# A decoder layer in fp32 on one core: casts begun one unit ahead, some low parts made by accumulating transfers, and eleven activations per feed-forward turned by transposing transfers

## The chip, the core and the metric

The kernel runs on one core of one Trainium2 chip. A core has five engines with their own instruction queues that meet through semaphores: TensorE (PE: matrix products; its weight loads are shown apart as PEld), VectorE (DVE), ScalarE (ACT), GpSimd (POOL) and SyncE (SP, which here only issues transfers). Sixteen DMA engines move data between device memory and on-chip memory, and between places in on-chip memory. The metric is device time of one execution in microseconds. All times are in us unless marked ns.

## The reference

One layer for 256 tokens of 2048 features, in float32:

```python
h = layer_norm(alpha * x + 0.5 * swiglu(x, w_ffn1_gu, w_ffn1_down))         # ffn 1, 2048 -> 2 x 5632 -> 2048
rq, rk, rv, rg, aq, ak, av, gate_r, gate_a = split(h @ w_in)
ret = (silu(rg) * group_norm(retention(rotary(rq), rotary(rk), rv))) @ w_ret_out
att = sliding_window_attention_with_sinks(rotary(aq), rotary(ak), av) @ w_att_out
h = layer_norm(alpha * h + (sigmoid(gate_r) * ret + sigmoid(gate_a) * att) @ w_mix_out)
h = layer_norm(alpha * h + 0.5 * swiglu(h, w_ffn2_gu, w_ffn2_down))         # ffn 2
h = layer_norm(alpha * h + sigmoid(h @ w_ple_gate) * (p @ w_ple_proj))
# swiglu(x, w_gu, w_down): g, u = split(x @ w_gu); return (silu(g) * u) @ w_down
```

Nearly all the work is products of 256 tokens with large weight matrices that are read once.

## The kernel before

**Three products for one.** Each fp32 operand is split into a high part (a cast to the type fp32r, `act.copy`, on ScalarE) and a low part (operand less high part, `dve.tensor_tensor`, on VectorE). `Sum.add` (L370 to L379) then issues three matmuls: low × high (L377), high × high (L378), high × low (L379).

**Units.** Weights come in chunks of 128 × 1024 floats (512 KB) by transfers from SP (L112). A plain unit (`Single`, "P", two per pair of chunks) is one chunk: load, cast (L98), subtraction (L99), then 12 matmuls of 512 columns. An S unit (`Seven`) takes a pair of chunks through Strassen's scheme: seven products for eight, 21 matmuls, for which VectorE forms four sums and more low parts (L174 to L185). A D unit (`Prepared`) has those sums written to device memory earlier, by VectorE in quieter stages (`sums_ahead`), and loads them.

**The planner.** `plan` lists the units in order. `fill` (L263) loads the next one while there is room in a budget of slots (`room["slots"]`, 24 in the feed-forwards' first products) and less than 90 matmuls are queued, and makes the next loaded one (cast and low parts) while less than 45 matmuls are ready. `take` hands a unit to TensorE, `done` gives its slots back and calls `fill`. Engines execute in the order in which the code is traced; a transfer also waits until the slot it writes has been released. All slots come from one pool of 46 of 4 KB per partition.

**Side jobs.** `later(n, job)` puts a job n places down a list; `run_side`, called after each chunk or S unit, runs the first entry. So `later(3, job)` runs behind the fourth next chunk.

**A feed-forward** (`ffn`, L898). The first product is done in 11 blocks of 512 columns (256 gate, 256 up). Block 0 has 16 plain chunks; the others follow an order of eight pairs, `PPSSPSSP` for ffn 1 (L860), with D units in blocks 1, 2, 3, 4, 5 and 7 of ffn 2 (L859). Four PSUM banks (`g`, `u`) collect the direct products and four more (`s0` to `s3`) Strassen's sums. Behind the last S unit `seven_common` (L479) folds the latter on VectorE (L483 to L486), a last plain pair follows, then VectorE adds the direct sums (L972), ScalarE applies Silu (L973) and VectorE multiplies (L974, by `later(1)`) into a tile `evw` of [128 tokens, 2, 512]. The down projection needs it transposed: `turned` (L908, by `later(2)`) transposes eight 128 × 128 squares on TensorE (L916) into two PSUM banks and copies them out by ScalarE (L918). `convert` (L922) splits the result, `seven_forms` makes sums of it; both are used from block 10 on.

**Between the feed-forwards** lies the mixer. Its value product uses the order `PSPSPSPS` (L1084); behind it the q and k projections of retention (`rqk`, L1178 to L1181) begin, whose matmuls stand at L328 (high) and L336 (low).

Of the kernel before, what the change touches and what calls it, by code (L numbers as in the profile page):

```python
# [10 lines left out]
I32 = mybir.dt.int32  # L11
AF = mybir.ActivationFunctionType
# [3 lines left out]
P = 128  # L16
S = 256
# [38 lines left out]
def layer(ctx: ExitStack, tc: tile.TileContext, io):  # L56
# [44 lines left out]
    class Chunk:  # L101
# [18 lines left out]
        def make(self):  # L120
            self.make_hi()
            split(self.hi, self.lo, self.raw)
# [6 lines left out]

        def columns(self, kk):  # L130
            return self.of(self.hi, kk), self.of(self.lo, kk)

    class Single:
# [9 lines left out]

        def make(self):
            self.chunk.make()

    class Seven:
# [4 lines left out]
        loads, makes, keeps, time = 2, 6, 7, 21  # L152
# [6 lines left out]

        def make(self):  # L160
# [4 lines left out]

            def shaped(x):
                return x.rearrange("p (g n) -> p g n", g=2) if a.paired else x

            t1, t3, t2, t4 = (shaped(x) for x in (u[:, 0], u[:, 1], v[:, 0], v[:, 1]))
            a.make_hi()  # L170
            both = slot([P, 2, 512], F32R, "b" + nm)
            h22, l22 = shaped(both[:, 0]), shaped(both[:, 1])
            uh, ul, vh, vl = (slot([P, 2, 512], F32R, w + nm) for w in ("hu", "lu", "hv", "lv"))
            act.copy(a.hi, a.raw)  # L174
            act.copy(h22, b22)
# [4 lines left out]
            dve.tensor_tensor(a.lo, a.raw, a.hi, ALU.subtract)  # L180
            dve.tensor_tensor(t4, t2, b21, ALU.add)  # L181
            act.copy(vh, v)  # L182
            dve.tensor_tensor(l22, b22, h22, ALU.subtract)
            dve.tensor_tensor(ul, u, uh, ALU.subtract)  # L184
            dve.tensor_tensor(vl, v, vh, ALU.subtract)  # L185
            self.b11, self.b21 = a.columns(0), a.columns(1)
            self.b22 = both[:, 0], both[:, 1]
# [5 lines left out]
    class Prepared:  # L193
# [3 lines left out]

        def __init__(self, key, other):
            self.key, self.other = key, other
# [10 lines left out]

        def make(self):
            a = self.a
            a.make()
            self.b11, self.b21 = a.columns(0), a.columns(1)
            both = slot([P, 2, 512], F32R, "b" + a.name)
            self.b22 = both[:, 0], both[:, 1]
            split(*(both[:, e].rearrange("p (g n) -> p g n", g=2) for e in range(2)), self.b)
            uh, ul, vh, vl = self.sums
            self.t1, self.t3 = ((uh[:, e], ul[:, e]) for e in range(2))
            self.t2, self.t4 = ((vh[:, e], vl[:, e]) for e in range(2))  # L220
# [42 lines left out]
    def fill(must=False):  # L263

        while True:
            queued = sum(u.time for u in ready)
            left = room["slots"] - room["used"]
            wanted = must and not ready or not room["quiet"] and queued < room["ahead"]
            if loaded and wanted and loaded[0].makes <= left:
                u = loaded.pop(0)  # L270
                u.make()
                room["used"] += u.keeps - u.loads
                ready.append(u)
                continue
            first = loaded[0] if loaded else plan[0] if plan else None
            queued += sum(u.time for u in loaded)
            if plan and queued < room["far"] and plan[0].loads + first.makes <= left:
                u = plan.pop(0)
                u.load()
                room["used"] += u.loads  # L280
                loaded.append(u)
                continue
            return

    def make_next():
        u = loaded.pop(0)
        assert u.makes <= room["slots"] - room["used"]
        u.make()
        room["used"] += u.keeps - u.loads
# [109 lines left out]
    def block_units(units, keys):  # L399

        for kind, p in units:
            if kind == "P":
                plan.extend(Single(keys(n, p)) for n in range(2))
# [3 lines left out]
    def block(name, units, keys, lhs, forms, sums, fold, before=None):  # L407


        sevens = [p for kind, p in units if kind != "P"]  # L410
        if sevens:
            p1, p6, p7, q5 = (Sum(bank(f"{name}s{j}"), len(sevens)) for j in range(4))
        for j, (kind, p) in enumerate(units):
            if before is not None:
                before(j)
            if kind == "P":
# [21 lines left out]
            if p == sevens[-1]:  # L438
                fold(p1.ap, p6.ap, p7.ap, q5.ap)

# [26 lines left out]
    def units_of(order, sevens, ahead=()):  # L467
# [3 lines left out]
        of = {"S": sevens, "D": ahead, "P": plain}  # L471
# [383 lines left out]
    def gu_units(name, j):  # L855
# [4 lines left out]
        return units_of("PPSSPSSP", SEVEN)  # L860
# [37 lines left out]
    def ffn(name, i, ht, norm, keep, residual, keepers, away):  # L898
# [9 lines left out]
        def turned(j, v):  # L908

            raw = slot([P, 4, S], F32, f"{name}a{j}")  # L910
            raws.append(raw)
            ps = banks(f"{name}t{j}")
            for k in range(4):
                for t in range(2):
                    at = slice(k % 2 * S + t * P, k % 2 * S + t * P + P)
                    pe.transpose(ps[k // 2][:, at], v[:, t, k * P : (k + 1) * P], ident)  # L916
            for h in range(2):
                act.copy(raw[:, 2 * h : 2 * h + 2], ps[h].rearrange("p (b n) -> p b n", b=2))  # L918
# [8 lines left out]
        for j in range(KF // 4):  # L927
            pg, pu = banks(f"{name}g{j}"), banks(f"{name}u{j}")
            units = gu_units(name, j)
            n_of = {(0, 0): KD, (0, 1): KD, (1, 0): KD, (1, 1): KD}  # L930
            for kind, p in units:
                if kind != "P":
# [34 lines left out]
            block(f"{name}{j}", units, gu_keys(name, j), rhs, forms, sums, lambda *a: got.extend(seven_common(*a)), before)  # L967
# [13 lines left out]
            later(2, lambda j=j, v=v: turned(j, v))  # L981
# [102 lines left out]
    VALUE_UNITS = units_of("PSPSPSPS", (0, 1, 2, 3))  # L1084
# [32 lines left out]
    def mixers(ht, norm, residual, keepers, away):  # L1117
# [57 lines left out]
        slots_for_weights(14)  # L1175
        rq[:] = [slot([P, 4, S], F32, f"rq{j}") for j in range(2)]
# [630 lines left out]
```

## Time and profile before

| | |
|---|---|
| three runs | 2278.32 median, 2276.88 to 2278.9 |
| the profiled execution | 2278.22, span of its instructions 2276.4 |
| granted TensorE clock, mean | 0.998 |
| PE / DVE / ACT / POOL busy | 2260.9 / 2031.3 / 1241.1 / 2.3 |
| matmuls | 10467 |
| moved by DMA | 515.72 MB, nearly all on SP's queue |

The profile is of one execution. A matmul's duration in it (0.39 us for 512 columns) overlaps with the next one's; the distance between starts says what one costs. "idle before" and "<-" name the time that an engine stood before an instruction and what ended it. Tile names are cut of their numbers: `f1g` are the gate sums of ffn 1, `f1t` the banks of a turn, `hf_gu` and `lf_gu` the high and low part of a chunk, `rf_gu` the chunk as loaded, `huf_gu`, `hvf_gu` and `luf_gu`, `lvf_gu` the parts of an S unit's sums. A row of stretches gives, between two times, busy time and instructions of each engine, the granted clock, the DMA engines' busy share and GB/s.

### The profile page before, as it was taken

To read this page: it belongs to the slowest core of one execution; us is meant where nothing else is said; L and a number is where in the kernel's file an instruction comes from. 1 tells how busy PE (TensorE), PEld (TensorE's weight loads), DVE (VectorE), ACT (ScalarE), POOL (GpSimd) and SP (SyncE) were. 2 spreads that over 40 slices of the span, in tenths; PEclk is the share of its full clock that TensorE was granted. 3 is DMA by queue.
4 is the path that set the end of the run, shared out by engine and by line. 5 is a ranking of instruction groups with operands and counts; after the bars stand their busy time and mean duration, and the time that the engine had idled before them with its cause. 6 is when DMAs were issued, how large, how long until landed. Compare 5 with 4: busy or idle time off the path is not lost.

```text
span 2276.4 us, 29157 instructions
## 1 busy us (share of the span) xinstructions
PE 2260.9 (99%) x10467; PEld 1873.9 (82%) x10467; DVE 2031.3 (89%) x2664; ACT 1241.1 (55%) x1514; POOL 2.3 (0%) x9
## 2 busy tenths in 40 slices
PE   9999999999999999999999999999999999999998
PEld 8888888888888888888778888888888888888887
DVE  7999999999989999888789788689898899889887
ACT  5655655656554644445666544455555556555543
POOL 0000000000000000000000000000000000000000
PEclk9999999999999999999999999999999999999999
DMA  8666665665677778866446568787877766556772
GB/s 309 207 197 196 196 213 176 198 209 190 212 286 263 258 243 309 269 225 217 147 148 223 193 208 293 271 286 253 287 260 226 254 206 205 194 188 215 290 270 74
DMA packets 211129, 515.72 MB, mean 227 GB/s; under 512 B 16412, under 2 KB 20892, under 8 KB 210984
## 3 DMA queue, kind: packets, MB, share of 16 engines
q1 hardware_dynamic: 209000, 511.28, 66.4%
q10 hardware_dynamic: 1984, 2.58, 0.4%
q8 instruction: 82, 1.34, 0.2%
q14 instruction: 63, 0.52, 0.1%
HBM read 484.43 MB, written 29.36 MB: 226 GB/s over the span
## 4 chain that ended last, share of the span: by engine, by line
PE 91%; DVE 8%; issue 1%; ACT 0%; ACTq 0%; POOL 0%; DVEq 0%; POOLq 0%
PE rqk L328 3%; PE f1g L379 2%; PE f1g L377 2%; PE f1g L378 2%; PE f2g L379 2%; PE f2g L378 2%; PE f1u L379 2%; PE f2g L377 2%; PE f1u L377 2%; PE f1u L378 2%; PE f2u L379 2%; PE f2u L377 2%; PE f2u L378 2%; PE aqk L328 2%; PE f2d L379 2%; PE f1d L378 2%
## 5 line engine op out<-in xcount | busy, mean ns | idle before, releaser
L99 DVE TENSOR_TENSOR lf_gu<-rf_gu,hf_gu 128x1024 fp32r<-128x1024 f32 (+1 forms) x192 | 223.7, 1210 | 15.2 <-ACT hf_gu L98 14.6
L98 ACT CAST hf_gu<-rf_gu 128x1024 fp32r<-128x1024 f32 (+1 forms) x192 | 190.3, 1041 | 20.7 <-DMA rf_gu<-in_f_gu 19.0
L99 DVE TENSOR_TENSOR lw_in_f<-rw_in_f,hw_in_f 128x1024 fp32r<-128x1024 f32 x132 | 158.0, 1219 | 25.1 <-ACT hw_in_f L98 24.9
L99 DVE TENSOR_TENSOR lf_down<-rf_down,hf_down 128x1024 fp32r<-128x1024 f32 x124 | 147.3, 1221 | 25.4 <-ACT hf_down L98 24.9
L98 ACT CAST hf_down<-rf_down 128x1024 fp32r<-128x1024 f32 x124 | 125.2, 1049 | 34.9 <-DMA rf_down<-in_f_down 15.4
L179 ACT CAST huf_gu<-uf_gu 128x1024 fp32r<-128x1024 f32 x76 | 80.1, 1054 | 109.5 <-DVE uf_gu L177 79.4
L98 ACT CAST hw_in_f<-rw_in_f 128x1024 fp32r<-128x1024 f32 x132 | 132.8, 1051 | 9.8 <-DMA rw_in_f<-in_w_in_f 3.1
L182 ACT CAST hvf_gu<-vf_gu 128x1024 fp32r<-128x1024 f32 x76 | 80.1, 1054 | 96.9 <-DVE vf_gu L181 93.0
L184 DVE TENSOR_TENSOR luf_gu<-uf_gu,huf_gu 128x1024 fp32r<-128x1024 f32 x76 | 92.7, 1220 | 0.0
L185 DVE TENSOR_TENSOR lvf_gu<-vf_gu,hvf_gu 128x1024 fp32r<-128x1024 f32 x76 | 92.7, 1220 | 0.0
L180 DVE TENSOR_TENSOR lf_gu<-rf_gu,hf_gu 128x1024 fp32r<-128x1024 f32 x76 | 92.7, 1220 | 0.0
L377 PE MATMUL f1g<-hf_gu,xt 128*128 128x512 f32 x232 | 90.4, 390 | 0.0
L379 PE MATMUL f1g<-lf_gu,xt 128*128 128x512 f32 x232 | 90.4, 389 | 0.0
L378 PE MATMUL f1g<-hf_gu,xt 128*128 128x512 f32 x232 | 90.3, 389 | 0.0
L973 ACT ACTIVATE eve<-eve 128x1024 f32<-128x1024 f32 x20 | 21.2, 1061 | 114.9 <-DVE eve L972 114.9
L377 PE MATMUL f2g<-hf_gu,ht 128*128 128x512 f32 x214 | 83.5, 390 | 0.0
L379 PE MATMUL f2g<-lf_gu,ht 128*128 128x512 f32 x214 | 83.3, 389 | 0.0
L378 PE MATMUL f2g<-hf_gu,ht 128*128 128x512 f32 x214 | 83.3, 389 | 0.0
L174 ACT CAST hf_gu<-rf_gu 128x1024 fp32r<-128x1024 f32 x76 | 79.6, 1047 | 4.0 <-DMA rf_gu<-in_f_gu 4.0
L377 PE MATMUL f1u<-hf_gu,xt 128*128 128x512 f32 x192 | 75.6, 394 | 0.0
L379 PE MATMUL f1u<-lf_gu,xt 128*128 128x512 f32 x192 | 74.8, 390 | 0.0
L378 PE MATMUL f1u<-hf_gu,xt 128*128 128x512 f32 x192 | 74.8, 389 | 0.0
(1572 smaller groups left out, 6865.7 us busy)
## 6 DMA issues: line engine op xcount, KB each, us to landing
rf_gu<-in_f_gu SPq DMA_DIRECT2D x360, 512.0 KB
rf_down<-in_f_down SPq DMA_DIRECT2D x176, 512.0 KB
rw_in_f<-in_w_in_f SPq DMA_DIRECT2D x148, 512.0 KB
rw_rv<-in_w_rv SPq DMA_DIRECT2D x32, 512.0 KB
rw_ret<-in_w_ret SPq DMA_DIRECT2D x32, 512.0 KB
rw_mix<-in_w_mix SPq DMA_DIRECT2D x32, 512.0 KB
rw_pg<-in_w_pg SPq DMA_DIRECT2D x32, 512.0 KB
rw_att<-in_w_att SPq DMA_DIRECT2D x16, 512.0 KB
```

What stands on the lines that cost most here:

```text
L98: act.copy(dst_hi, src)
L99: (lo_engine or dve).tensor_tensor(dst_lo, src, dst_hi, ALU.subtract)
L174: act.copy(a.hi, a.raw)
L179: act.copy(uh, u)
L180: dve.tensor_tensor(a.lo, a.raw, a.hi, ALU.subtract)
L182: act.copy(vh, v)
L184: dve.tensor_tensor(ul, u, uh, ALU.subtract)
L185: dve.tensor_tensor(vl, v, vh, ALU.subtract)
L328: pe.matmul(ps[f], hi[:, kk, f * P : (f + 1) * P], rhs(k), start=k == 0, stop=k == n_k - 1,)
L377: pe.matmul(o, al, bh, start=first, stop=False)
L378: pe.matmul(o, ah, bh, start=False, stop=False)
L379: pe.matmul(o, ah, bl, start=False, stop=self.left == 0)
```

## The change

1. **Casts one unit ahead.** A unit gets a step `begin` ahead of `make`: the casts of the chunks as loaded. `make_next` begins the unit at hand if that has not been done, then the next one (a T unit already when it is third in line) if there are slots, and then makes its low parts.
2. **T units.** In the orders without D units, `PPSSPSSP` becomes `PTSSPSST`. The second chunk of a T pair is `Transferred`: ScalarE writes the negated high part into the low part's slot, and a transfer from GpSimd's queue adds the chunk to it in place, which leaves the low part; the cast to the high part comes in `make`.
3. **Turns.** `turned` now copies the tile's 16-bit halves apart on ScalarE (`later(3)`); `turn`, three steps on, issues one transposing transfer of 128 × 2048 two-byte elements from SP; `join`, four steps on, copies the halves together on ScalarE. No transposes on TensorE and no PSUM banks.
4. **Banks and the value block.** For even blocks from 2 the four banks of Strassen's sums are asked for ahead of `g` and `u`. The value product's order becomes `PSPSSPSP`, and four banks named `pass` are asked for, and not used, behind it.

```diff
     class Chunk:
-        def make(self):
-            self.make_hi()
-            split(self.hi, self.lo, self.raw)
+        def begin(self):
+            self.hi = slot(list(self.raw.shape), F32R, "h" + self.name)
+            act.copy(self.hi, self.raw)
+        def end(self):
+            self.lo = slot(list(self.raw.shape), F32R, "l" + self.name)
+            dve.tensor_tensor(self.lo, self.raw, self.hi, ALU.subtract)
+        def transfer(self):
+            self.lo = slot(list(self.raw.shape), F32R, "l" + self.name)
+            act.mul(self.lo, self.raw, -1.0)
+            pool.dma_start(self.lo, self.raw.bitcast(F32R), accum_op=ALU.add)
...
+    class Unit:
+        begun, begins, lead = False, 1, 1
...
+    class Transferred(Single):
+        lead = 3
+        def begin(self):
+            self.chunk.transfer()
+        def make(self):
+            self.chunk.begin()
...
     class Seven(Unit):
+        def begin(self):
+            a, b = self.a, self.b
+            a.begin()
+            self.both = slot([P, 2, 512], F32R, "b" + a.name)
+            self.h22, self.l22 = (a.shaped(self.both[:, e]) for e in range(2))
+            act.copy(self.h22, b.of(b.raw, 1))
...
+    def begin(u):
+        u.begun = True
+        u.begin()
+        u.loads, u.makes = u.loads + u.begins, u.makes - u.begins
+        room["used"] += u.begins
+
     def make_next():
         u = loaded.pop(0)
         assert u.makes <= room["slots"] - room["used"]
+        if not u.begun:
+            begin(u)
+        room["used"] += u.keeps - u.loads
+        for j, v in enumerate(loaded[:3]):
+            if not v.begun and j < v.lead and v.begins + (loaded[0].makes if j else 0) <= room["slots"] - room["used"]:
+                begin(v)
         u.make()
-        room["used"] += u.keeps - u.loads
         ready.append(u)
...
-        return units_of("PPSSPSSP", SEVEN)
+        return units_of("PTSSPSST", SEVEN)
...
         def turned(j, v):
+            parts = slot([P, 2, 2, 512], U16, f"{name}w{j}")
+            words = v.bitcast(U16).rearrange("p t (n w) -> p w t n", w=2)
+            for w in range(2):
+                act.copy(parts[:, w], words[:, w])
+            later(3, lambda: turn(j, parts))
+
+        def turn(j, parts):
+            turns = slot([P, 16, P], U16, f"{name}t{j}")
+            sync.dma_start_transpose(turns, parts.rearrange("p w t n -> p (w t n)"))
+            later(4, lambda: join(j, turns))
+
+        def join(j, turns):
             raw = slot([P, 4, S], F32, f"{name}a{j}")
             raws.append(raw)
-            ps = banks(f"{name}t{j}")
-            for k in range(4):
-                for t in range(2):
-                    at = slice(k % 2 * S + t * P, k % 2 * S + t * P + P)
-                    pe.transpose(ps[k // 2][:, at], v[:, t, k * P : (k + 1) * P], ident)
-            for h in range(2):
-                act.copy(raw[:, 2 * h : 2 * h + 2], ps[h].rearrange("p (b n) -> p b n", b=2))
+            words = raw.bitcast(U16).rearrange("p k (t n w) -> p w k t n", t=2, w=2)
+            turns = turns.rearrange("p (w t k) n -> p w k t n", w=2, t=2)
+            for w in range(2):
+                act.copy(words[:, w], turns[:, w])
...
+            extra = seven_banks(f"{name}{j}") if j and j % 2 == 0 else None
             pg, pu = banks(f"{name}g{j}"), banks(f"{name}u{j}")
...
-            later(2, lambda j=j, v=v: turned(j, v))
+            later(3, lambda j=j, v=v: turned(j, v))
...
-    VALUE_UNITS = units_of("PSPSPSPS", (0, 1, 2, 3))
+    VALUE_UNITS = units_of("PSPSSPSP", (0, 1, 2, 3))
...
         slots_for_weights(14)
+        for j in range(4):
+            bank(f"pass{j}")
```

More of the change, by code (lines that the diff above doesn't have):

```diff
@@ L11 @@
 I32 = mybir.dt.int32
+U16 = mybir.dt.uint16
 AF = mybir.ActivationFunctionType
@@ L965, in before @@
                     convert(u // 2 - 2)
[L967 removed]
+            block(f"{name}{j}", units, gu_keys(name, j), rhs, forms, sums, lambda *a: got.extend(seven_common(*a)), before, extra)
             if got:
```

76 lines of the change are left out of this document (36 added, 40 removed).

## The prediction

> **What bounds the kernel now.** I read the page first, then who made TensorE wait, then the instructions around one turn in order of time, then the stretches of the first feed-forward.
>
> ```profile
> span 2276.4 us, 29157 instructions
> ...
> PE 2260.9 (99%) x10467; PEld 1873.9 (82%) x10467; DVE 2031.3 (89%) x2664; ACT 1241.1 (55%) x1514; POOL 2.3 (0%) x9
> ...
> q1 hardware_dynamic: 209000, 511.28, 66.4%
> ...
> PE 91%; DVE 8%; issue 1%; ACT 0%; ACTq 0%; POOL 0%; DVEq 0%; POOLq 0%
> ```
>
> TensorE is busy for all but 15.5 us of the span and is 91% of the chain that ended last. A gain must therefore come from fewer or shorter TensorE instructions, and every other engine only has to keep up. The list of TensorE's waits is short:
>
> ```profile
> PE rqk L328 <- DVE evw L483: 2.8, 1, 2.8
> PE f2t L916 <- DVE evw L974: 2.4, 9, 0.3
> PE f1t L916 <- DVE evw L974: 2.4, 9, 0.3
> ```
>
> Two of the three rows are the transposes of `turned` (L916), which the change takes off TensorE; the third is the start of the q and k projections behind the value block, whose order it alters. In order of time, a turn in a later block of the first feed-forward (start, duration):
>
> ```profile
> 182.11 0.39 PE L379 MATMUL f1g<-lf_gu,xt 128*128 128x512 f32 x1
> ...
> 183.47 0.39 PE L379 MATMUL f1g<-lf_gu,xt 128*128 128x512 f32 x1
> 184.13 1.07 PE L916 MATMUL f1t<-ident,evw 128*128 128x128 f32 x8 [0.27 <-DVE evw L974]
> 184.95 0.48 PE L377 MATMUL f1u<-hf_gu,xt 128*128 128x512 f32 x1
> 185.27 0.39 PE L378 MATMUL f1u<-hf_gu,xt 128*128 128x512 f32 x1
> ```
>
> and one without the wait, for block 0:
>
> ```profile
> 57.43 0.39 PE L379 MATMUL f1g<-lf_gu,xt 128*128 128x512 f32 x1
> 57.66 1.03 PE L916 MATMUL f1t<-ident,f1v 128*128 128x128 f32 x8
> 58.45 0.47 PE L377 MATMUL f1u<-hf_gu,xt 128*128 128x512 f32 x1
> 58.77 0.39 PE L378 MATMUL f1u<-hf_gu,xt 128*128 128x512 f32 x1
> ```
>
> Durations overlap, so cost is read from starts. Six matmuls take 183.47 − 182.11 = 1.36, or 0.2267 us each. Around the first turn, L379 to L378 takes 185.27 − 183.47 = 1.80 us where two intervals would take 0.45: the turn costs **1.35 us**. Without the wait it is 58.77 − 57.43 − 0.45 = **0.89 us**.
>
> What must keep up, by stretches (length; then busy us of PE, PEld, DVE, ACT, POOL; granted clock; DMA share; GB/s):
>
> ```profile
> 139.60:181.80 42.20, 41.93 (x190) 34.59 (x189) 41.16 (x50) 24.54 (x29) 0.00 (x0) 1.00 0.62 188
> 181.80:223.90 42.10, 41.83 (x190) 34.47 (x189) 41.05 (x50) 24.38 (x29) 0.00 (x0) 1.00 0.61 188
> ...
> 1573.00:1614.00 41.00, 40.74 (x184) 33.59 (x183) 40.09 (x50) 23.52 (x28) 0.00 (x0) 1.00 0.82 291
> 1614.00:1656.00 42.00, 41.73 (x189) 34.38 (x189) 36.69 (x44) 22.99 (x28) 0.00 (x0) 1.00 0.73 248
> ```
>
> The first two are one block of ffn 1 each: VectorE works 41.1 of 42.2 us. It runs only a little ahead of TensorE. The last low part of a block's fourth S unit is made, and used, here:
>
> ```profile
> 204.60 1.22 DVE L185 TENSOR_TENSOR lvf_gu<-vf_gu,hvf_gu 128x1024 fp32r<-128x1024 f32 x1
> ```
>
> ```profile
> 209.32 0.39 PE L379 MATMUL f14s<-lvf_gu,f1fh 128*128 128x512 f32 x1
> ```
>
> It ends at 205.82, 3.5 us before its use: that is the smallest lead in a block.
>
> **The change part by part.**
>
> *Turns.* There are 22 (11 blocks in each ffn). 18 run behind `evw` (two rows of 9 waits), 4 without a wait (blocks 0 and 10 of each ffn, counted at block 0's price). TensorE loses 18 × 1.35 + 4 × 0.89 = 24.3 + 3.6 = **27.9 us** of work. Nothing on the chain takes its place if the new route is in time, since the results are first read in the last block (`convert`) and in the down projection.
>
> The new route costs ScalarE four copies of 1024 two-byte elements in place of two of 512 floats, and SP one transposing transfer:
>
> ```profile
> L98 ACT CAST hf_gu<-rf_gu 128x1024 fp32r<-128x1024 f32 x64 | 63.2, 1051 | 0.0
> L182 ACT CAST hvf_gu<-vf_gu 128x1024 fp32r<-128x1024 f32 x32 | 33.8, 1055 | 41.1 <-DVE vf_gu L181 41.1
> L179 ACT CAST huf_gu<-uf_gu 128x1024 fp32r<-128x1024 f32 x32 | 33.7, 1054 | 50.3 <-DVE uf_gu L177 33.9 <-PE f1t L916 16.4
> ...
> L918 ACT COPY f1a<-f1t 128x512 f32<-128x512 f32 x16 | 8.5, 584 | 0.0
> L973 ACT ACTIVATE eve<-eve 128x1024 f32<-128x1024 f32 x8 | 8.5, 1061 | 45.8 <-DVE eve L972 45.8
> ```
>
> (ScalarE in eight blocks: count, busy, mean ns, idle before, by whom.) No row has a two-byte copy; 584 ns (half the elements) and 1051 ns (as many) bound it, and I take 1.05. Each block then has 4.2 − 1.2 = +3.0 us of ScalarE. The split waits for `evw` on ScalarE; behind it stand only casts of later units, and the wait that L179 had for the transposes (16.4 us) goes.
>
> The transposing transfer moves 512 KB. Queue 1 carries 511.28 MB in 66.4% of 16 engines over 2276.4 us, which is 24,184 engine-us, 47.3 per MB: 512 KB alone on 16 engines is 24.8 / 16 = 1.55 us. That is the low end. For the high end let it be cut into 2048 pieces that each cost a mean packet of that queue, 24,184 / 209,000 = 0.116 us: 2048 × 0.116 / 16 = 14.8 us, and 39 us if it only gets the 0.38 of the engines that a block leaves idle. I take 4 us, nearer the low end because the bytes are the same. Its cover is the way from `turn` (behind the eighth chunk step) to `join` (the thirteenth): S, S, T, T, P are 21 + 21 + 12 + 12 + 12 = 78 matmuls, 17.7 us. SP's loads queue behind it while it waits for the split, but the split is traced 66 matmuls (15 us) earlier, so I charge nothing; unmet, each load behind it comes late by the remaining wait.
>
> [...]
>
> *Transferred chunks.* T units stand in ten blocks of ffn 1 and four of ffn 2 (blocks 6, 8, 9, 10): 28 chunks. Each takes one subtraction of 1024 columns off VectorE:
>
> ```profile
> L99 DVE TENSOR_TENSOR lf_gu<-rf_gu,hf_gu 128x1024 fp32r<-128x1024 f32 x8 | 9.3, 1220 | 0.2 <-ACT hf_gu L98 0.2
> ```
>
> 9.3 / 8 = 1.16 us, so 2.3 us a block: VectorE goes to 38.8 against a TensorE block of 42.2 − 1.35 = 40.8. ScalarE gains two scalings of 1.05 us (with the copies: 24.5 + 3.0 + 2.1 = 29.6 of 40.8), POOL two issues on an empty queue. The six ahead-blocks of ffn 2 have no T; there VectorE needs (40.09 + 36.69) / 2 = 38.4 per pair member against about 41.5 − 1.35 = 40.1, so it keeps up as well.
>
> The accumulating transfer reads source and destination and writes: one to three passes of 512 KB, 1.55 to 4.65 us alone, 12.2 us if it gets only the idle 0.38. I take 6. Followed through `take`, `fill` and `make_next` with 24 slots, a block's two T chunks are begun 60 and 66 matmuls before their first matmul; less the scaling that is 12.5 and 13.9 us, **13.2 on average**. Even the high end fits, barely. Cost: nothing; uncovered, L379 waits.
>
> *Casts one unit ahead.* VectorE's waits for its casts vanish, but TensorE's waits list shows none that they caused: nothing. The casts ask for their load 12 or 21 matmuls (2.7 or 4.8 us) earlier; the L98 row above has 0.0 idle, so the loads have been early enough by some margin that no row states. From nothing to ScalarE standing 2 us a block, inside its idle time; priced in the second rival.
>
> *Value block and banks.* The fold gets a plain pair behind it. Before:
>
> ```profile
> 796.08 3.49 DVE L99 TENSOR_TENSOR lw_in_f<-rw_in_f,hw_in_f 128x1024 fp32r<-128x1024 f32 x3
> ...
> 800.22 2.79 PE L328 MATMUL rqk<-ht,hw_in_f 128*128 128x512 f32 x7 [2.76 <-DVE evw L483]
> ```
>
> ```profile
> 760.00:815.00 55.00, 51.46 (x235) 42.27 (x234) 54.59 (x69) 31.64 (x37) 0.00 (x0) 0.97 0.82 283
> ...
> 801.00:804.30 3.30, 3.30 (x12) 2.83 (x11) 3.30 (x6) 0.79 (x1) 0.00 (x0) 0.50 0.99 395
> ```
>
> Behind the 2.76 us wait the granted clock is 0.50 for 3.3 us, which costs 1.65. At most 4.4 us is to be had. But VectorE is busy 54.59 of 55 us there: two S units side by side ask it for their sums earlier, so the wait mostly moves into the value block. From 0 to −4.4; I take the clock alone, **−1.6**. The unused `pass` banks and `extra` change which banks follow which; if every even block waited at its start for the last two sums of L972, that would be some 1.4 us × 10. I take nothing and keep it in the second rival.
>
> Sum, against the profiled execution's own time of 2278.2 (span 2276.4 and 1.8 outside it; the median of the runs is 2278.3): 2278.2 − 27.9 − 1.6 = **2248.7, say 2249 us**.
>
> **The rivals.**
>
> 1. *ScalarE's extra work reaches VectorE.* Five us more a block stand in the same queue as the casts of u and v, for which VectorE waits. VectorE has 40.8 − 38.8 = 2.0 us of room; all 5.1 us landing in its way would cost 3.1 us in each of 14 blocks, 43 us (2292), half of it 2270. For it: `join` falls where the S units' casts begin. Against it: ScalarE stands idle 17.7 of 42.2 us, and the plain casts now lie a unit earlier.
>
> 2. *Slower: the accumulating transfer is late.* Place: L379 on a T chunk's low part. Price: 28 × (latency − 13.2 us). It decides from 13.2 + 29.5 / 28 = 14.3 us upward; at 16 us it is 2249 + 78 = 2327. For it: the high end (12.2) is close, POOL's queue has never been used here, and it shares engines with loads at 0.62. Against: it needs all three passes at the leftover rate.
>
> 3. *Slower: the transposing transfer is late.* ScalarE stops at `join`, casts and then VectorE's sums are late. It decides beyond cover and lead, 17.7 + 3.5, plus the gain of 1.5 a block: 22.7 us; at 25 us, 20 × 3.8 = 76 us more than forecast, 2325. [...]
>
> 4. *It doesn't do what it says:* slots run out, T chunks are begun only when made, 33 to 36 matmuls (7.5 to 8.2 us) ahead; then rival 2 decides from about 7.8 us.
>
> **How the numbers follow.** About 0.2% (4.6 us) either way is what a measurement of this kernel can tell from no change. Forecast 0.65, its own range 2245 to 2256 (the whole 4.4 at the value block, or 1.4 us in some blocks at the banks); rival 1 0.15, spread over 2256 to 2292; rivals 2 and 4 together 0.13; rival 3 0.07. Rival 1 gives 0.09 to faster, 0.03 to the same and 0.03 to slower; rivals 2 to 4 give 0.02 to faster, 0.02 to the same and 0.16 to slower. Faster 0.76, same 0.05, slower 0.19. The range 2243 to 2284 holds the forecast, most of rival 1 and the mild ends of the others, 0.8 in all.
>
> **What would show it.** Right: no L916, blocks of ffn 1 some 40.8 us apart, VectorE near 38.8 in them, no TensorE wait on POOL or a transfer, no clock of 0.50 at the q and k projections. Wrong: TensorE waits at L379 of f1g or f1u for a transfer (rival 2), ScalarE waits at the joining copies (3), or VectorE waits for huf or hvf (1).

## The result, and the profile after

The changed kernel takes **2260.61 us** (median of four runs, 2256.68 to 2262.82) against 2277.82 for the kernel before beside it (2276.88 to 2278.9): a ratio of 0.9921, 95% interval 0.9909 to 0.9933. It is faster by 17.2 us; the forecast was 29. The profiled execution took 2261.72. From its page:

```profile
span 2259.6 us, 28888 instructions
...
PE 2243.5 (99%) x10291; PEld 1856.3 (82%) x10291; DVE 1995.2 (88%) x2636; ACT 1345.4 (60%) x1586; POOL 26.7 (1%) x37
...
q1 hardware_dynamic: 254760, 522.82, 68.7%
q0 software_dynamic: 4032, 14.68, 3.5%
...
PE 89%; DVE 5%; DMA 3%; issue 1%; ACT 1%; SPq 0%; ACTq 0%; DVEq 0%
DMA rf_gu<-in_f_gu 3%; PE rqk L369 3%; PE f1g L420 2%; PE f1g L419 2%; PE f1g L418 2%; PE f1u L419 2%; PE f1u L418 2%; PE f1u L420 2%; PE f2g L419 2%; PE f2g L418 2%; PE f2g L420 2%; PE f2u L419 2%; PE f2u L418 2%; PE f2u L420 2%; PE aqk L369 2%; PE f2d L418 2%
...
L124 ACT CAST hf_gu<-rf_gu 128x1024 fp32r<-128x1024 f32 x264 | 271.2, 1047 | 40.7 <-DMA rf_gu<-in_f_gu 37.5
L124 ACT CAST hf_down<-rf_down 128x1024 fp32r<-128x1024 f32 x150 | 153.1, 1050 | 66.8 <-DMA rf_down<-in_f_down 51.9
...
lf_gu<-rf_gu POOLq DMA_DIRECT2D x28, 512.0 KB, 8.0
```

The 176 transposes are gone (10467 − 10291 matmuls), VectorE is relieved by 36 us, and something new is on the chain: 3% of it is loads of weights (`rf_gu`). ScalarE now stands before its casts for 37.5 and 51.9 us until a load has landed (19.0 and 15.4 in the kernel before). That alone need not cost anything: the version without transferred chunks, below, has 36.2 and 41.0. TensorE's waits (total, times, longest) are no longer a list of transposes but of low parts that VectorE delivers late, at the ninth and tenth block of a feed-forward (`f19s`, `f210s`, `f1d`) and at the norm ahead of feed-forward 2 (`lnps`):

```profile
PE lnps L670 <- DVE mixy L658: 1.9, 2, 1.5
PE f210s L420 <- DVE luf_gu L216: 1.4, 1, 1.4
...
PE rvss L420 <- DVE luw_rv L216: 1.3, 1, 1.3
PE f1d L420 <- DVE lf_down L128: 0.9, 1, 0.9
PE f19s L420 <- DVE luf_gu L216: 0.7, 1, 0.7
```

**Where the gain went** is read by comparing when TensorE first touches the same tile in two profiled executions. The table is worked out from those starts: what TensorE gained on the kernel before in a stretch, in us (negative: lost). The other columns are experiments, told below.

```
                                    changed  turns   turns on  no trans-  no casts  begun 2  best
stretch (first matmul into a tile)           alone   TensorE   ferred     ahead     ahead    version
ffn 1, block 4 to 5                   1.36    0.12     0.00      1.36       1.36     1.37     1.37
ffn 1, block 9 to 10                 -0.05    0.12     0.01      1.18      -2.63     1.37     1.37
ffn 1, block 10 into down product    -0.43   -4.83     0.00     -0.80      -1.33     0.56     0.89
value block into the gate product     2.91    1.56     2.94      2.89       2.62     2.95     2.94
last mixing block to ffn 2           -3.89    0.03    -2.27     -2.01       0.03    -3.94    -0.12
ffn 2, block 5 to 9                   3.74   -7.93     0.01      4.02      -4.30     4.10     3.59
ffn 2, block 9 into down product     -2.24    0.24     0.00      1.02      -2.18     1.19     2.26
whole                                16.98   -0.16     0.15     23.81       9.90    23.54    27.77
```

A block in which nothing waits gains 1.36 us, the price put on a turn. Blocks 9 and 10 of both feed-forwards lose some 8 us in all (ffn 1: 1.42 + 1.32; ffn 2: 0.79 behind block 8, 4.50 behind block 10), and the norm ahead of feed-forward 2 loses 3.9.

One such loss, followed back through the trace (start, duration). SyncE's queue:

```profile
1863.36 0.37 SPq L113 DMA_DIRECT2D rf_gu<-in_f_gu  x1
1863.82 3.41 SPq L962 DMA_TRANSPOSE f2t<-f2w  x1
1867.34 11.18 SPq L113 DMA_DIRECT2D rf_gu<-in_f_gu  x7
```

ScalarE:

```profile
1876.93 1.06 ACT L133 ACTIVATE lf_gu<-rf_gu 128x1024 fp32r<-128x1024 f32 x1 [3.94 <-DMA rf_gu<-in_f_gu]
...
1878.83 0.57 ACT L526 COPY eve<-f29s 128x512 f32<-128x512 f32 x1
```

VectorE, and TensorE 33 us later:

```profile
1879.44 0.69 DVE L527 TENSOR_TENSOR evw<-eve,f29s 128x512 f32<-128x512 f32 x1 [4.17 <-ACT eve L526]
```

```profile
1912.56 0.19 PEld L420 LDWEIGHTS f210s<-lf_gu,ht 128*128 128x128 f32 x1 [0.92 <-DVE lf_gu L128]
```

Behind this wait and the next one (1.4 us, for `luf_gu`) the granted clock is 0.50 for 3.3 us, which is some 1.7 of the 4.50 us lost here (a row of a stretch):

```profile
1916.50:1919.80 3.30, 3.30 (x10) 2.52 (x9) 3.28 (x4) 3.30 (x5) 0.00 (x0) 0.50 1.03 318
```

The *issue* of one transposing transfer occupies SyncE's queue for 3.41 us (an ordinary load: 0.37). The loads behind it go out late. The second of them is the chunk of a T unit, which is begun three units ahead: its scaled copy (L133) stands on ScalarE for 3.94 us, and the copy that opens the block's fold (L526) stands behind it. VectorE waits 4.17 us for the fold, from 1879 on has no pause, and TensorE meets the low parts late. All of it, per execution (waits of ScalarE and of VectorE; then SyncE's issues, min/median/max ns):

```profile
ACT lf_gu L133 <- DMA rf_gu<-in_f_gu: 20.1, 9, 4.3
```

```profile
DVE evw L527 <- ACT eve L526: 23.7, 10, 4.5
```

```profile
L962 SPq DMA_TRANSPOSE f1t<-f1w x11: 2875/3450/4654, 68.5 to 474.1; - x11
```

```profile
L962 SPq DMA_TRANSPOSE f2t<-f2w x11: 1787/6862/9352, 1537.8 to 1939.8; - x11
```

### The profile page after: what moved, and what is told of

Read it like the earlier page. It is cut to its first block, busy times and chain, and to the rows that moved or that the text cites. A ratio compares the mean times of both kernels' runs of the same rounds, so it can differ in the third digit from the quotient of the medians.

```text
span 2259.6 us, 28888 instructions
## 1 busy us (share of the span) xinstructions
PE 2243.5 (99%) x10291; PEld 1856.3 (82%) x10291; DVE 1995.2 (88%) x2636; ACT 1345.4 (60%) x1586; POOL 26.7 (1%) x37
## 3 DMA queue, kind: packets, MB, share of 16 engines
q1 hardware_dynamic: 254760, 522.82, 68.7%
## 4 chain that ended last, share of the span: by engine, by line
PE 89%; DVE 5%; DMA 3%; issue 1%; ACT 1%; SPq 0%; ACTq 0%; DVEq 0%
DMA rf_gu<-in_f_gu 3%; PE rqk L369 3%; PE f1g L420 2%; PE f1g L419 2%; PE f1g L418 2%; PE f1u L419 2%; PE f1u L418 2%; PE f1u L420 2%; PE f2g L419 2%; PE f2g L418 2%; PE f2g L420 2%; PE f2u L419 2%; PE f2u L418 2%; PE f2u L420 2%; PE aqk L369 2%; PE f2d L418 2%
## 5 line engine op out<-in xcount | busy, mean ns | idle before, releaser
L128 DVE TENSOR_TENSOR lf_gu<-rf_gu,hf_gu 128x1024 fp32r<-128x1024 f32 x236 | 281.6, 1218 | 16.0 <-ACT hf_gu L124 15.0
L124 ACT CAST hf_gu<-rf_gu 128x1024 fp32r<-128x1024 f32 x264 | 271.2, 1047 | 40.7 <-DMA rf_gu<-in_f_gu 37.5
L124 ACT CAST hf_down<-rf_down 128x1024 fp32r<-128x1024 f32 x150 | 153.1, 1050 | 66.8 <-DMA rf_down<-in_f_down 51.9
L128 DVE TENSOR_TENSOR lf_down<-rf_down,hf_down 128x1024 fp32r<-128x1024 f32 x150 | 178.0, 1219 | 14.2 <-ACT hf_down L124 6.5
L128 DVE TENSOR_TENSOR lw_in_f<-rw_in_f,hw_in_f 128x1024 fp32r<-128x1024 f32 x140 | 166.4, 1217 | 3.1 <-ACT hw_in_f L124 3.1
L124 ACT CAST hw_in_f<-rw_in_f 128x1024 fp32r<-128x1024 f32 x140 | 142.0, 1051 | 33.2 <-DMA rw_in_f<-in_w_in_f 24.9
L418 PE MATMUL f2u<-hf_gu,ht 128*128 128x512 f32 x168 | 65.7, 391 | 0.0
L420 PE MATMUL f2u<-lf_gu,ht 128*128 128x512 f32 x168 | 65.4, 389 | 0.0
L419 PE MATMUL f2u<-hf_gu,ht 128*128 128x512 f32 x168 | 65.4, 389 | 0.0
```

The source lines that it names most:

```text
L124: act.copy(self.hi, self.raw)
L128: dve.tensor_tensor(self.lo, self.raw, self.hi, ALU.subtract)
L418: pe.matmul(o, al, bh, start=first, stop=False)
L419: pe.matmul(o, ah, bh, start=False, stop=False)
L420: pe.matmul(o, ah, bl, start=False, stop=self.left == 0)
```

## The experiments

All ratios are to the kernel before on the same chip, with 95% intervals.

### One part alone, one part undone

**Turns alone**: no casts ahead, no transferred chunks, the old value block, no `pass` and `extra` banks.

```diff
-            if not v.begun and j < v.lead and v.begins + (loaded[0].makes if j else 0) <= room["slots"] - room["used"]:
+            if not v.begun and v.lead > 1 and j < v.lead and v.begins + (loaded[0].makes if j else 0) <= room["slots"] - room["used"]:
...
-        return units_of("PTSSPSST", SEVEN)
+        return units_of("PPSSPSSP", SEVEN)
...
-            extra = seven_banks(f"{name}{j}") if j and j % 2 == 0 else None
+            extra = None
...
-    VALUE_UNITS = units_of("PSPSSPSP", (0, 1, 2, 3))
+    VALUE_UNITS = units_of("PSPSPSPS", (0, 1, 2, 3))
...
-        for j in range(4):
-            bank(f"pass{j}")
```

> The kernel before with one part of the change alone: the turns by transposing transfers (parting copies, transfer, joining copies, and the three steps). No transferred chunks, no casts ahead, the old order of the value block, the old PSUM banks.
> Theory A (SyncE's queue is held: each transposing transfer stands 2.9 to 9.4 us in the load queue, the loads behind it land late, ScalarE stands before their casts, VectorE falls behind): the lateness comes with the turns alone, and VectorE has 41.1 us of work a block of feed-forward 1 against 40.8 us of TensorE, so nothing makes it up: 2262 to 2270 us.
> Theory B (the transferred chunks cause the lateness, by a scaled copy that stands in ScalarE's order three units early): it is gone here, and VectorE's 41.1 us alone sets the blocks, so 42.15 - 41.1 = 1.05 us for each of 18 turns and 0.89 us for four: 2278 - 22 = about 2256 us.
> Theory C (the casts ahead cause it): as B, about 2256 us, and the norm ahead of feed-forward 2 loses nothing (by A and B too where the casts ahead alone are behind that loss).

Measured: 2279.61 us, ratio 1.0003 (0.9994 to 1.0011): **no gain at all**. All three theories were too high on the gain. Two blocks of feed-forward 1, by stretches (length; busy PE, PEld, DVE, ACT, POOL), and VectorE's wait over four blocks:

```profile
254.00:296.00 42.00, 41.34 (x182) 33.58 (x181) 40.91 (x50) 27.70 (x30) 0.00 (x0) 1.00 0.67 209
296.00:338.00 42.00, 41.34 (x181) 33.61 (x180) 40.90 (x50) 27.73 (x30) 0.00 (x0) 1.00 0.72 208
```

```profile
DVE lf_gu L128 <- ACT hf_gu L124: 3.8, 4, 1.0
```

VectorE is busy for 40.9 us a block and stands 1.0 us for a cast: 41.9 together, in a block of 42.0. With the transposes gone, VectorE's wait for its casts, which had cost nothing, is the bound, and TensorE gains 0.12 a block. The 1.56 us in the table's value row are no gain of the turns: the wait at the q and k projections is as long as before (2.79 us for 2.76), but the clock, which was 0.50 for 3.3 us behind it in the kernel before, is 1.00 here (last section).

**Turns on TensorE**, two steps behind as before and without the `extra` banks; the rest of the change is kept.

```diff
         def turned(j, v):
-            parts = slot([P, 2, 2, 512], U16, f"{name}w{j}")
...
+            for k in range(4):
+                for t in range(2):
...
+                    pe.transpose(ps[k // 2][:, at], v[:, t, k * P : (k + 1) * P], ident)
...
-            extra = seven_banks(f"{name}{j}") if j and j % 2 == 0 else None
+            extra = None
...
-            later(3, lambda j=j, v=v: turned(j, v))
+            later(2, lambda j=j, v=v: turned(j, v))
```

> The changed kernel with its turns back on TensorE, as in the kernel before (two steps behind, two PSUM banks); transferred chunks, casts ahead and the new value block stay.
> Theory A (held load queue): no lateness in the feed-forwards; the 27.6 us of turns come back, the 2.9 us of the value block stay gained, and about 3.9 us are lost at the norm ahead of feed-forward 2 if the casts ahead do that: 2275 to 2279 us.
> Theories B and C (transferred chunks or casts ahead bring the lateness): the losses of the changed kernel stay and the turns come on top: 2260.6 + 27.6 = about 2285 to 2288 us, unless TensorE's turns leave VectorE the time to make them up (then as A).

Measured: 2278.66 us, ratio 1.0002 (0.9993 to 1.0011). As theory A has it, no block loses anything. But a block is 1.36 us longer for TensorE here, so VectorE has time to make lateness up, and the run can't acquit the transferred chunks: ScalarE still stood 16.3 us at their scaled copies, with no transposing transfer in the kernel:

```profile
ACT lf_gu L133 <- DMA rf_gu<-in_f_gu: 16.3, 9, 2.6
```

So the early copy alone can make most of that wait (20.1 us in the changed kernel). The run also shows 2.3 us lost at the norm without any transposing transfer.

**No transferred chunks.**

```diff
-        return units_of("PTSSPSST", SEVEN)
+        return units_of("PPSSPSSP", SEVEN)
```

> The changed kernel without the transferred chunks: all plain chunks of the feed-forward blocks have their low parts subtracted by VectorE (41.1 us a block of feed-forward 1, against 40.8 us of TensorE).
> Theory A (held load queue): the lateness stays and VectorE can't make it up: 16 blocks of 0.3 us and more, 2265 to 2275 us.
> Theory B (transferred chunks bring the lateness): the losses at blocks 9 and 10 (1.4 + 1.3 + 4.5 us) go and VectorE's bound costs 0.3 us a block: 2255 to 2260 us.
> Theory C: 2262 to 2266 us, the bound alone.

Measured: **2254.81 us**, 0.9896 (0.9880 to 0.9911), runs of 2254.36 to 2255.47, all below those of the changed kernel. Theory B, just below its range, since the 0.3 us a block that it took for VectorE's bound are not lost. The queue is held as long here (3.42 and 6.86 us at the median of the two feed-forwards), so that alone costs little. VectorE has no room, and needs none, for its wait for the casts is gone:

```profile
250.00:291.00 41.00, 41.00 (x183) 33.95 (x182) 40.80 (x49) 27.60 (x30) 0.00 (x0) 1.00 0.71 218
```

It is busy 40.80 of 41.00 us, and TensorE still has 41.00 of 41.00. What transferred chunks could buy is what this version still misses: 0.19 us a block late in feed-forward 1 (1.18 for 1.37) and, by the last column of the table, 2.9 us at the two down products (-0.80 for 0.89, 1.02 for 2.26). As the change places them they cost 5.8 us instead.

**No casts ahead.**

```diff
-            if not v.begun and j < v.lead and v.begins + (loaded[0].makes if j else 0) <= room["slots"] - room["used"]:
+            if not v.begun and v.lead > 1 and j < v.lead and v.begins + (loaded[0].makes if j else 0) <= room["slots"] - room["used"]:
```

> The changed kernel without the casts one unit ahead: plain and seven-product units are cast where they are made, as before; the transferred chunks are still begun up to three units ahead.
> Theory A with the norm's loss put down to the casts ahead: the 3.9 us at the norm ahead of feed-forward 2 come back and the rest stays: about 2257 us.
> Theory C (the casts ahead, and the slots they hold, are what makes the loads late): the losses of blocks 9 and 10 go too, 2248 to 2252 us.
> The other side (the casts ahead are what hides ScalarE's waits from VectorE): VectorE's stalls return in each block, 2262 to 2275 us.

Measured: 2270.91 us, 0.9964 (0.9952 to 0.9977): "the other side". VectorE's waits for casts of `rf_gu` chunks come back, 51.6 us where the changed kernel has 15.0:

```profile
DVE lf_gu L128 <- ACT hf_gu L124: 51.6, 49, 4.1
```

The casts ahead are worth 10 us. Yet the norm ahead of feed-forward 2 loses nothing here, nor in the first run: the 2 to 3.9 us lost there come with the casts ahead.

### Taking the collision apart

**The same transferred chunks elsewhere.**

```diff
-        return units_of("PTSSPSST", SEVEN)
+        return units_of("PPSSTSST", SEVEN)
```

> The changed kernel with the first transferred chunk of each block moved from the second plain unit to the third (the order of the units stays): as many transferred chunks (28), the same scaled copies, transposing transfers and held queue; only, the chunk begun three units ahead is no longer one whose load is issued right behind the transposing transfer.
> Theory B+A (a collision: the transferred chunk's scaled copy stands in ScalarE's order for a load that the transposing transfer held up, and the fold and VectorE stand behind it): the 20.1 us of ScalarE's waits at the scaled copies fall below 5, the losses of blocks 9 and 10 go: 2250 to 2254 us, below the version without transferred chunks (2254.8), since VectorE has 2.3 us a block less.
> Rival (a transferred chunk costs its ScalarE copy and the slots that it holds three units early, whichever chunk it is): 2258 to 2262 us, as the changed kernel.

Measured: 2257.67 us, 0.9901 (0.9887 to 0.9916), four runs of 2252.05 to 2258.55, so the median lies between the two forecasts. ScalarE's waits at the scaled copies fell as predicted, from 20.1 us:

```profile
ACT lf_gu L133 <- DMA rf_gu<-in_f_gu: 0.6, 2, 0.3
```

and block 10 of feed-forward 2 loses nothing (−0.02 for −4.50). But in the profiled execution (2258.07) blocks 7 and 8 of feed-forward 1 lose 5.5 us on something else: at 317.6 a transposing and an accumulating transfer start within 0.1 us of each other and end within 0.2 us of each other at 334.6, 17 us later; loads issued meanwhile take 15.1 to 16.2 us, and TensorE waits 1.4 us for the accumulating transfer, the only execution up to here in which it did:

```profile
PE f1u L420 <- DMA lf_gu<-rf_gu: 1.4, 1, 1.4
```

**The turn two steps later.**

```diff
-            later(3, lambda: turn(j, parts))
+            later(5, lambda: turn(j, parts))
```

> The changed kernel with the transposing transfer issued five steps behind the parting copies in place of three (the joining copies stay four steps behind it): the loads of the transferred chunk and of the seven-product unit behind it are then issued ahead of it.
> Theory B+A (collision of the held queue with the scaled copy): as above from the other side, 2250 to 2255 us; the loads that now stand behind the transfer had 6 to 12 us in hand.
> Rival (price of the transferred chunk itself): 2258 to 2262 us.
> A held queue that hits other loads as hard: 2258 us and above, with ScalarE's waits at other casts.

Measured: 2280.36 us, 1.0005 (0.9987 to 1.0023), from 2266.76 to 2290.02. The third theory's bound holds, and ScalarE's waits at the plain casts of `rf_gu` do grow, from 37.5 to 47.6 us, but no theory had what costs most. ScalarE's waits at the scaled copies shrank to 4.0 us, while the profiled execution shows the pair of long transfers of the run above, only longer. SyncE, and TensorE's waits:

```profile
1743.82 12.34 SPq L962 DMA_TRANSPOSE f2t<-f2w  x1
```

```profile
PE f2u L420 <- DMA lf_gu<-rf_gu: 18.0, 2, 14.5
```

Landing times, worked out from the landing records of each transfer (us from issue to last landing, min / median / max):

```
                        transposing (22)      accumulating (28)
changed kernel          4.3 /  6.6 / 12.0     6.0 / 8.0 / 10.4
no transferred chunks   4.3 /  5.8 / 10.8     none
begun 2 ahead           4.4 /  7.2 / 10.7     5.8 / 7.3 / 10.1
T moved                 4.5 /  7.7 / 17.1     4.8 / 7.4 / 16.9
turn two steps later    4.5 / 10.7 / 25.9     5.8 / 7.3 / 24.2
late turn, no T         4.3 /  7.3 / 10.4     none
```

**The late turn without transferred chunks.**

```diff
-        return units_of("PTSSPSST", SEVEN)
+        return units_of("PPSSPSSP", SEVEN)
-            later(3, lambda: turn(j, parts))
+            later(5, lambda: turn(j, parts))
```

> The changed kernel without transferred chunks (2254.8 us), with the transposing transfer issued five steps behind the parting copies in place of three.
> Theory (with both kinds of transfer in flight at once each takes 14 to 26 us instead of 6 to 10; that made the version with the late turn and with transferred chunks 2280 us): without the accumulating transfers there is nothing to collide with: 2253 to 2258 us.
> Rival (the late turn alone, with its queue held 7 us in place of 3.4, makes the loads late): 2265 us and above.

Measured: 2266.44 us, 0.9947 (0.9934 to 0.9959). The long transfers are gone (last line of the table), as the theory has it; the 2253 to 2258 it predicted are missed, though, and the rival's number came out for another reason than the rival gives. The three loads behind each late transfer landed 5.8 to 9.9 us before their casts in feed-forward 1. What is late is ScalarE's cast of `u`, for which VectorE waits 1.1 us in every block of 42 us:

```profile
DVE luf_gu L216 <- ACT huf_gu L211: 4.5, 4, 1.3
```

(four blocks). The later joining copies stand in ScalarE's order where VectorE's casts stood; that they are what delays `huf_gu` was not tried by itself. Against this run, the transferred chunks cost 2280.4 − 2266.4 = 14 us with the late turn.

**Begun two units ahead, not three.**

```diff
     class Transferred(Single):
-        lead = 3
+        lead = 2
```

> The changed kernel with transferred chunks begun two units ahead in place of three, in their old places.
> Theory B (the scaled copy stands in ScalarE's order for a load that has not landed): one unit later the load is there, the 20.1 us of waits at the scaled copies go under 8: 2252 to 2257 us.
> Rival (the accumulating transfer, 8.0 us from issue to landing, then lands too late for TensorE): 2262 us and above, with TensorE's waits at transferred chunks.

Measured: **2255.58 us**, 0.9898 (0.9884 to 0.9911), runs of 2255.25 to 2256.26. Theory B: waits at the scaled copies 2.9 us for 20.1, TensorE never waits for a transfer, and blocks 9 and 10 of feed-forward 1 get their gain back (1.37 for −0.05, 0.56 for −0.43). One unit of lead made 5 us.

```profile
ACT lf_gu L133 <- DMA rf_gu<-in_f_gu: 2.9, 7, 1.0
```

### The norm ahead of feed-forward 2, and the best version

**Casts ahead off from the fourth mixing block** until block 0 of feed-forward 2, first without transferred chunks, then together with the moved ones.

```diff
-            if not v.begun and j < v.lead and v.begins + (loaded[0].makes if j else 0) <= room["slots"] - room["used"]:
+            if not v.begun and j < v.lead and room["casts"] and v.begins + (loaded[0].makes if j else 0) <= room["slots"] - room["used"]:
 ...
                 slots_for_weights(24)
+                room["casts"] = True
...
         slots_for_weights(26, 136, 160)
+        room["casts"] = False
```

> The changed kernel without transferred chunks (2254.8 us) and with no cast begun ahead from the last mixing block to the end of the norm ahead of feed-forward 2; elsewhere the casts stay one unit ahead.
> Theory (a cast begun ahead holds a slot early, so the loads of feed-forward 2's first units are issued later, and the norm's VectorE work stands behind their casts): the 2.0 us lost there come back: 2252 to 2253 us.
> Rival (the loads there are bound by what the DMA engines move, so that they can't follow TensorE's gain): no change, 2254 to 2256 us.

Measured: 2256.56 us, 0.9904 (0.9892 to 0.9917): not better than the 2254.81 without the edit; the norm loses 3.99 us. Some 3.4 us (2 × 1.7) of its profiled execution (2257.95) are lost to two stretches at half clock, one in the value block and one at the norm, which the version without the edit doesn't have.

> The changed kernel with both: the first transferred chunk of a block in the third plain unit, and no casts ahead at the norm ahead of feed-forward 2.
> Both theories right: 2247 to 2251 us, below both kernels.
> The transferred chunk's price is its own: 2255 to 2259 us.

Measured: 2253.25 us, 0.9896 (0.9883 to 0.9909), between the two forecasts. Blocks 8 to 10 now lose nothing (1.37 and 0.89 throughout); the norm still loses 3.69. So the rule was at fault, or the place. The loads' order told which: in the kernel without casts ahead the load of the last embedding chunk (`rw_pp`) waits for no slot, here it still does, because of casts begun in the mixing block before. The next run turns them off one block earlier:

```diff
...
             if blk == 2:
                 load_for_norm(1)
+                room["casts"] = False
...
```

> The changed kernel with the first transferred chunk of a block in the third plain unit, and no casts ahead from the third mixing block (blk == 2) to the end of the norm ahead of feed-forward 2, so that the load of the last embedding chunk no longer waits for a slot there.
> Theory (a slot held by a cast begun ahead pushes that load, and all behind it, 10 us back): the 3.7 us lost at that norm come back: 2248 to 2251 us.
> Rival (the norm's loss is not the slots'): as with the casts turned off one block later, 2252 to 2255 us.

Measured: **2250.51 us, 0.9880 (0.9864 to 0.9895)**, runs of 2249.97 to 2254.28: below the kernel before by 28.3 us and, by intervals that don't meet, below the changed kernel. The norm loses 0.12 us. SyncE's two `rw_pp` loads, in the changed kernel, then here:

```profile
1430.42 10.08 SPq L113 DMA_DIRECT2D rw_pp<-in_w_pp  x2
1440.59 9.13 SPq L113 DMA_DIRECT2D rf_gu<-in_f_gu  x7
```

```profile
1427.73 0.86 SPq L113 DMA_DIRECT2D rw_pp<-in_w_pp  x2
1437.72 9.04 SPq L113 DMA_DIRECT2D rf_gu<-in_f_gu  x7
```

In the changed kernel the second of them waits 9.3 us for a slot (1430.9 to 1440.2), and each weight chunk behind it goes out one place later; with no cast begun ahead from one mixing block earlier on, it waits for none. The norm's work stands on VectorE behind the chunks' low parts.

**The value block's adjacent pair at its end.**

```diff
-    VALUE_UNITS = units_of("PSPSSPSP", (0, 1, 2, 3))
+    VALUE_UNITS = units_of("PSPSPSSP", (0, 1, 2, 3))
```

> As i_best, and the value block's units in the order plain, seven, plain, seven, plain, seven, seven, plain: the two adjacent seven-product units stand last, where VectorE has had more time.
> If TensorE's waits in the value block (1.3 + 0.5 us) come from the place of the adjacent pair: 1.0 to 1.6 us below i_best.
> If they come with the pair wherever it stands: the same as i_best, or slower.

Measured: 2253.39 us, 0.9890 (0.9877 to 0.9904), from 2251.32 to 2257.97: not separable from the run before, and TensorE lost 3.07 us in the block in place of 1.64. The pair costs its wait wherever it stands: TensorE's waits in the block are 2.0 us in both, and the 1.4 us more that are lost here are about what the half clock behind them costs (half of 3.4 us):

```profile
781.90:785.20 3.30, 3.20 (x8) 2.43 (x8) 3.30 (x4) 3.30 (x5) 0.00 (x0) 0.50 0.08 32
```

The profiled execution (2257.97) has a long pair of transfers again (15.4 and 14.6 us), at block 8 of feed-forward 1.

## Why the prediction was right in sign and 12 us too low

- **Turns, −27.9 us: the price was right.** Blocks in which nothing waits gain 1.36 or 0.89 us (1.35 and 0.89 predicted). The transposing transfer took 4.3 to 12.0 us, median 6.6, where 4 was taken and 14.8 was the bound; its cover from issue to joining copy was 19.4 to 31.4 us, not 17.7; ScalarE never waited at the joining copies, so rival 3 did not occur.
- **"SP's loads queue behind it ... I charge nothing": the first step that failed, but cheap by itself.** Only the wait for the parting copies was looked at, not the issue itself, which holds the queue for 3.45 us at the median in feed-forward 1 and 6.86 in feed-forward 2. It is held as long without transferred chunks, and all that this version still loses against the forecast is 2254.8 − 2248.7 = 6.1 us, 2.0 of them at the norm.
- **"Even the high end fits, barely. Cost: nothing": the second, and the larger.** The accumulating transfer was as predicted (median 8.0 us for 6 taken and 12.2 at most; rivals 2 and 4 did not occur in the changed kernel). What was not priced is its *opening*: the scaled copy stands in ScalarE's in-order queue three units early and asks for a load that has not landed. In seven of its nine waits that load went out second behind a transposing transfer; but ScalarE stood 16.3 us there (20.1 in the changed kernel) without any such transfer, so how much the held queue adds is not settled. Without transferred chunks the kernel is 5.8 us faster, begun one unit later 5.0 us. Blocks 9 and 10 show it because VectorE comes to them with the least lead; that was not tried by itself.
- **Casts ahead, "nothing": wrong twice.** The reason given, that no TensorE wait came from VectorE's waits for casts, held for blocks of 42.2 us. Once the turns are gone it is those waits that decide: 10 us (2270.91 without the casts ahead). And they hold slots early: at the norm 3.9 us are lost, of which some 1.7 is the clock (0.50 for 3.4 us, below); turned off in time, 0.12 us are lost there in place of 3.69. The prediction did see that ScalarE might stand for loads, up to 2 us a block, but left the price to "the second rival", where none stands.
- **Value block and banks: −1.6 predicted, −2.9 found.** The wait at the projections and its half clock went (4.58 us gained); 1.67 came back as waits inside the block, as foreseen in kind. That the clock stayed at 1.00 behind those can't be counted on: the same waits (1.3, 0.5 and 0.2 us) were followed by half clock in the run without transferred chunks that turns the casts off at the norm, and there the block gained 1.34.
- **Rival 1** is nearest in its time (2256 to 2292) but not in its mechanism: VectorE's waits were for the fold's copy, not for `huf` or `hvf` (0.8 us in all), and ScalarE was late for want of loads, not for its own work. So the forecast's own range (2245 to 2256) was missed, and the wide one held thanks to room kept for something that did not happen.

Of the marks named ahead, those of "right" were all met: no transposes, blocks 40.8 us apart, VectorE at 38.3 of 41.0 us (near 38.8 of 40.8 was named), no TensorE wait on a transfer, no half clock at the projections. The list lacked the waits that came: ScalarE's for loads. Not settled: the one to two us that most versions lose between blocks 5 and 7 of feed-forward 2.

By the table's stretches the sum closes to about 1 us: 2278.2 − 27.9 − 2.9 = 2247.4; the losses of 8.0 (blocks 8 to 10), 3.9 (norm), 0.9 (blocks 5 to 7 of feed-forward 2) and 0.3 (at the attention value product) make 2260.5, and the execution took 2261.7. Of the rest 0.75 lies ahead of block 1, where block 0's turn should have given 0.89 and TensorE is only 0.14 us earlier, and 0.3 outside the span of the instructions; why the first is missing is not known.

## What to carry to other kernels

When TensorE loses work, the next engine's *period*, its waits included, can become the bound (VectorE's 41.9 us in a block of 42.0 with the turns alone): price the edit against busy time plus waits, since waits that cost nothing before may be the whole gain now (turns alone: 0 us; with the casts ahead and the value block's part: 24). An instruction moved earlier on an engine that works in order is also an earlier demand on everything it reads, and on a slot (the scaled copies begun three units ahead stood 20.1 us for loads, two units ahead 2.9); choose what to move by the slack of its load, and move it no further than its latency needs. Count the issue time of every new transfer in the queue that it shares (here 3.45 and 6.86 us at the median), not only its landing.

## What was unexpected of the hardware

- In the changed kernel a transposing transfer of 128 × 2048 two-byte elements held its issuing queue for 1.8 to 9.4 us, against a median of 0.33 us (`rf_down`) and 0.41 us (`rf_gu`) for loads of the same 512 KB, and added 2080 packets to its queue ((254,760 − 209,000) / 22).
- A transposing and an accumulating transfer in flight together mostly took no longer than apart: in eight of the kernels here 117 of 122 accumulating transfers that overlapped a transposing one landed within 12.2 us. The other five took 13.6 to 24.2 us, and each time its partner was long as well; of the 102 that met none, the slowest took 12.2. What sets off the long ones isn't known.
- The granted clock was 0.50 behind some short waits of TensorE and 1.00 behind a longer one (rows below), so in these traces the length of the wait does not decide it alone. In the changed kernel waits of 1.46 and 0.48 us at the norm, with 0.4 us of work between them, were followed by 0.50 for 3.4 us; 1.11 and 0.48 us, in the kernel without transferred chunks, left it at 1.00:

```profile
1462.50:1465.80 3.30, 3.30 (x9) 2.55 (x8) 2.64 (x5) 0.54 (x2) 0.00 (x0) 0.50 0.00 0
```

```profile
1460.00:1463.40 3.40, 3.30 (x17) 2.73 (x18) 3.33 (x7) 1.22 (x4) 0.00 (x0) 1.00 0.09 31
```

With the turns alone, waits of 1.38 and 0.17 us in block 10 of feed-forward 1 were followed by 0.50, and the 2.79 us at the q and k projections by 1.00:

```profile
460.70:464.00 3.30, 3.30 (x9) 2.53 (x9) 3.30 (x4) 3.30 (x5) 0.00 (x0) 0.50 0.81 242
800.50:804.00 3.50, 3.50 (x20) 3.02 (x20) 3.47 (x6) 0.31 (x1) 0.00 (x0) 1.00 1.00 396
```

What decides it is not shown. An estimate from these rows: 0.50 for 3.4 us costs 1.7 us, so a difference of that size between two executions can be this alone.
